# A hybrid decoder step: the values of an RWKV pair turned by two transpositions and one product, and two pairs of half-row products cut into column pieces

## The chip, the cores and the metric

The kernel runs on one core of a Trainium2 chip. The metric is device microseconds (us) for one execution of the whole program: the median of three runs, and beside it one more execution recorded by the hardware profiler, whose rows are quoted below. Less is better.

## The reference, cut to what matters

One trunk layer is computed for 256 prompt tokens and 8 x 8 sample tokens (320 columns in all), in fp32. All groups read one normalised input:

```
proj = rms_norm(x) @ w_in
y_rw = rwkv7_mix(p_rw)     # 12 heads x 64: S = S*w + (S a) b^T + v k^T ; y = S r ; then layer norm, bonus, gate
y_hg = hgrn2_mix(p_hg)     # 6 heads, state 128 x 128, S = exp(b_last) S + sum (k exp(b_last - b)) v^T
y_lru = rglru_mix(p_lru)   # 512 channels
x = x + concat(y_rw, y_hg, y_lru) @ w_out
x = x + (silu(conv(gate)) * val) @ ffn_w_down      # gate, val = rms_norm(x) @ ffn_w_up
```

In `rwkv7_mix` the decay w and the rate a come from `tanh(xw) @ rwkv_w2` and `xa @ rwkv_a2`, two products over 64 rows each. The head outputs, all new states and two final norms are returned.

## The kernel before, in words

**The stream of weight products.** Tokens lie along the columns, features on the 128 partitions. Every weight tile of 128 x 128 is used in three products, because the fp32 operands are split into a high and a low part: high weight with high input (L198), high weight with low input (L199), low weight with high input (L205). A chunk is eight such tiles: SyncE loads it into `raw` (L167), ScalarE (ACT) makes the high part `wh` (L173), VectorE (DVE) the low part `wl` (L174). There are three buffers of `raw`, `wh` and `wl` each, and chunks are split two ahead of their use. A chunk is 16 products of L198 and L199 in turn, then 8 of L205, into PSUM tile `acc`.

**The chains between them.** The three mixing groups are generators (`rwkv_operands` = queue f, `rwkv_chunks` = r, `rwkv_norm` = n, `hgrn_steps` = h, `lru_steps` = l). Each `yield` carries a delay, and `tick()` inside the weight product lets a chain go on when the planned clock has passed it. So pieces of these chains stand between the weight products on TensorE (PE), in an order that is set when the program is built. Pairs of RWKV heads (0 to 5) and HGRN heads (0 to 5) alternate, about 80 us for one of each. Within an engine everything runs strictly in the built order; the framework that records the program also chooses, by its own estimate of readiness, how the instructions of different chains lie on ACT and DVE. A chain's PSUM tiles `aux_r` are four banks used in turn: a product that takes a bank waits until the bank's last reader is done.

**The part around the change**, for pair p. PE: `L621` turns the values v of the pair (as four products of 64 columns with the identity); the norm chain of the pair before stands near it (L832 variance, L842 gate); then L631 (sample values), L640 and L647 (transpositions of BK and BKs), L656 and so on. ACT: L623 copies L621's result to `vsw`; L834 and L835 are Ln and Exp on the variance of the pair before; L934 and L935 are four Exp of the HGRN head; L632 to L634 copy the sample values to `vs` and `uv`; L642 copies the BK transposition to `bkt`, L838 finishes the norm. An ACT instruction whose function isn't in the table that is loaded has an `ACT_TABLE_LOAD` ahead of it. In pairs 1 to 5, L640's first product waits for L623 and its second for L834 (the last readers of the two banks that it takes), L647 waits for L634, and L656 for the first L642. Pair 0 has no norm chain ahead of it.

**Elsewhere.** L482 are two products over 64 rows each (rows 0 to 63 give w, rows 64 to 127 give a) of 320 columns into two banks; L1048 are two over 64 rows each of 512 columns into two banks, for the sample states of an HGRN head. In pair p, the block inverse `U` is built by 30 small DVE instructions (L611, L613), written out and read back by SyncE (L614, L615), and turned by L686. A plain fp32 product takes two PE instructions in the trace, a transposition one.

## Time and profile before

| | |
|---|---|
| three runs | 1625.08, 1626.22, 1627.49 us; median 1626.22 |
| profiled execution | 1627.56 us, of which the span from first to last instruction 1625.8 |
| granted TensorE clock, mean | 0.997 |
| busy share of the span | PE 99%, weight loads on PE 95%, DVE 60%, ACT 50%, GpSimd 9% |
| HBM | 146 GB/s over the span |

PE spans are pipelined: a weight product is shown for 0.31 us, while the next starts 0.147 us after it, so PE counts as idle only when a wait is longer than what is still in flight. Distances between starts say more than durations do. In waits and timelines, `PEld` is the loading of the stationary operand, which runs ahead of the product, and "idle before, releaser" names what ended a wait.

### The profile page before, as it was taken

Reading aid. Unit: us, or ns where it says so; the run is one execution under the profiler, and the core shown is the slowest. Engines: PE = TensorE matmul, PEld = TensorE weight load, DVE = VectorE, ACT = ScalarE, POOL = GpSimd, SP = SyncE. Lnnn points to the kernel's source line nnn. Section 1 sums busy time; section 2 is a strip of 40 time slices with the busy share of each in tenths; the row PEclk is TensorE's granted clock in tenths of the full one; section 3 lists DMA queues with packets and bytes.
Section 4 is the critical chain, followed back from the end, with each engine's and each line's share of the span. In section 5 each row is a group of like instructions: output and inputs, shape, how many; then the busy total and the mean of one; then the engine's idle time right before and its main releaser. Section 6 shows DMA issues by size and latency. Waiting matters only on the chain.

```text
span 1625.8 us, 29013 instructions
## 1 busy us (share of the span) xinstructions
PE 1601.6 (99%) x11478; PEld 1548.6 (95%) x11478; DVE 973.9 (60%) x1965; ACT 809.6 (50%) x1280; POOL 144.7 (9%) x364
## 2 busy tenths in 40 slices
PE   9999999999999999999999999999999999999996
PEld 8888989898989999999999999999999999999996
DVE  7786878777776765555555554343455555554444
ACT  7766766676766964443434343323334343344442
POOL 2101111111111300001111110000011110000000
PEclk9999999999999999999999999999999999999998
DMA  8444343444344554454445444555444444445553
GB/s 266 154 132 135 117 141 120 128 120 136 114 135 122 168 169 150 151 158 148 151 148 156 145 153 144 147 152 149 155 151 154 146 153 145 155 146 156 149 151 109
DMA packets 87791, 238.91 MB, mean 147 GB/s; under 512 B 16712, under 2 KB 31096, under 8 KB 87656
## 3 DMA queue, kind: packets, MB, share of 16 engines
q1 hardware_dynamic: 81496, 221.01, 44.4%
q0 software_dynamic: 4576, 14.16, 2.6%
q8 instruction: 90, 1.47, 0.4%
q10 hardware_dynamic: 1584, 1.89, 0.3%
q14 instruction: 45, 0.37, 0.1%
HBM read 225.66 MB, written 11.37 MB: 146 GB/s over the span
## 4 chain that ended last, share of the span: by engine, by line
PE 85%; ACT 7%; DVE 4%; DMA 2%; issue 2%; SPq 0%; POOL 0%; DVEq 0%; ACTq 0%
PE acc L198 26%; PE acc L205 26%; PE acc L199 26%; DVE wl L174 1%; PE aux_r L703 1%; PE aux_h L914 1%; ACT wh L173 1%; DMA raw<-in_w_in 1%; ACT L935 0%; ACT L893 0%; ACT L1023 0%; DVE x L1289 0%; PE aux_r L656 0%; PE aux_r L729 0%; DMA mskf<-in_msk 0%
## 5 line engine op out<-in xcount | busy, mean ns | idle before, releaser
L173 ACT CAST wh<-raw 128x1024 fp32r<-128x1024 f32 (+2 forms) x412 | 421.6, 1025 | 542.8 <-PE acc L199 338.2
L198 PE MATMUL acc<-xh,wh 128*128 128x320 f32 x2192 | 661.0, 315 | 0.0
L199 PE MATMUL acc<-xl,wh 128*128 128x320 f32 x2192 | 648.2, 309 | 0.0
L174 DVE TENSOR_TENSOR wl<-raw,wh 128x1024 fp32r<-128x1024 f32 (+2 forms) x412 | 489.9, 1190 | 224.5 <-ACT wh L173 113.1
L198 PEld LDWEIGHTS acc<-xh,wh 128*128 128x128 f32 x2192 | 411.7, 188 | 13.6 <-issue 10.7
L199 PEld LDWEIGHTS acc<-xl,wh 128*128 128x128 f32 x2192 | 411.7, 188 | 1.3
L205 PE MATMUL acc<-xh,wl 128*128 128x320 f32 x2192 | 372.6, 312 | 0.0
L205 PEld LDWEIGHTS acc<-xh,wl 128*128 128x128 f32 x2192 | 332.3, 188 | 2.8
L198 PE MATMUL acc<-hh,wh 128*128 128x320 f32 x704 | 207.9, 308 | 0.0
L199 PE MATMUL acc<-hl,wh 128*128 128x320 f32 x704 | 207.9, 308 | 0.0
L199 PEld LDWEIGHTS acc<-hl,wh 128*128 128x128 f32 x704 | 132.1, 188 | 0.0
L198 PEld LDWEIGHTS acc<-hh,wh 128*128 128x128 f32 x704 | 131.7, 187 | 0.0
L205 PE MATMUL acc<-hh,wl 128*128 128x320 f32 x704 | 118.8, 308 | 0.0
L1251 POOL COPY ncch<-fe 128x18 f32<-128x18 f32 x44 | 49.7, 1131 | 652.7 <-DVE fe L1250 652.7
L205 PEld LDWEIGHTS acc<-hh,wl 128*128 128x128 f32 x704 | 107.1, 187 | 0.0
L1261 DVE TENSOR_TENSOR fv<-acc,rstd 128x320 f32<-128x320 f32 x44 | 21.6, 492 | 98.5 <-PE acc L205 98.5
L1249 DVE TENSOR_TENSOR fe<-acc,rstd 128x256 f32<-128x256 f32 x44 | 18.7, 425 | 99.6 <-PE acc L205 99.6
L214 ACT CAST hh<-fv 128x320 fp32r<-128x320 f32 x44 | 20.3, 460 | 96.9 <-DVE fv L1263 96.9
L198 PE MATMUL acc<-yhl,wh 128*128 128x320 f32 x224 | 66.2, 310 | 0.0
L199 PE MATMUL acc<-yhl,wh 128*128 128x320 f32 x224 | 66.0, 307 | 0.0
L1256 DVE SCALAR_TENSOR_TENSOR fc<-fe,prm,fc 128x336 f32<-128x336 f32 x88 | 49.8, 566 | 1.6
L1254 ACT ACTIVATE fc<-fe,prm 128x336 f32<-128x336 f32 x44 | 29.4, 669 | 35.7 <-DVE fe L1250 35.7
(416 smaller groups left out, 1616.6 us busy)
## 6 DMA issues: line engine op xcount, KB each, us to landing
raw<-in_w_up SPq DMA_DIRECT2D x176, 512.0 KB, 3.5
raw<-in_w_in SPq DMA_DIRECT2D x100, 512.0 KB, 3.5
raw<-in_w_dn SPq DMA_DIRECT2D x64, 512.0 KB, 3.4
raw<-in_w_out SPq DMA_DIRECT2D x32, 512.0 KB, 3.6
raw<-in_w_dn SPq DMA_DIRECT2D x32, 384.0 KB, 3.0
out_s_hgrn<-hs POOLq DMA_DIRECT2D x12, 256.0 KB, 4.6
xr<-in_xT SPq DMA_DIRECT2D x16, 160.0 KB, 3.8
hs<-in_hs POOLq DMA_DIRECT2D x10, 256.0 KB, 4.2
```

The costliest lines, as they stand in the source:

```text
L173: S.copy(wh[:, ks, :], raws[n][:, ks, :])
L174: V.tensor_tensor(wl[:, ks, :], raws[n][:, ks, :], wh[:, ks, :].bitcast(F32), op=ALU.subtract)
L198: PE.matmul(ps[:, :T], wh[:, k, :], xh[k0 + k], start=st, stop=False)
L199: PE.matmul(ps[:, :T], wh[:, k, :], xl[k0 + k], start=False, stop=False)
L205: PE.matmul(ps[:, :T], wl[:, k, :], xh[k0 + k], start=False, stop=en)
L214: S.copy(xh, src)
L703: PE.matmul(ps[q, b * 64:(b + 1) * 64], lhs[q, b, q], r[q], start=True, stop=True)
L1249: V.tensor_tensor(e[:, 2:258], ps[:, 0:TP], rstd[:, 0:TP], op=ALU.mult)
L1251: G.tensor_copy(ncch[:, j], e[:, 248:EX].rearrange("p (b s) -> p b s", s=10)[:, :, 8:10])
L1254: S.activation(c[:, 0:N], e[:, 0:N], AF.Identity, scale=pc("fw", 3 * j), bias=pc("fb", j))
L1256: V.scalar_tensor_tensor(c[:, 0:N], e[:, m:m + N], pc("fw", 3 * j + m), c[:, 0:N], op0=ALU.mult, op1=ALU.add)
L1261: V.tensor_tensor(val, ps[:, :T], rstd, op=ALU.mult)
```

## The change

It does three things. (1) The values are turned by one transposition of columns 64 to 191 (128 x 128), one of columns 192 to 255 into partitions 0 to 63, and one product with the identity for columns 0 to 63 into partitions 64 to 127. The two upper blocks then lie in swapped places, so that `vsw` is filled by three copies on ACT (the lower 64 partitions at once, the upper ones block by block) in place of one. (2) L482 becomes four products of 160 columns, (3) L1048 four of 256 columns, the two row halves in turn for each column piece.

```diff
         ps_w, ps_a = aux_r(), aux_r()
-        for n, ps in enumerate((ps_w, ps_a)):
-            PE.matmul(ps[:, :T], lw[half[n], n, :], lora[half[n], :], start=True, stop=True)
+        for c in (slice(0, T // 2), slice(T // 2, T)):
+            for n, ps in enumerate((ps_w, ps_a)):
+                PE.matmul(ps[:, c], lw[half[n], n, :], lora[half[n], c], start=True, stop=True)
...
         ps = aux_r()
-        for c in range(4):
-            PE.matmul(ps[half[1 - c % 2], (c // 2) * P:(c // 2 + 1) * P], v[:, c * 64:(c + 1) * 64], ident,
-                      start=True, stop=True)
-        S.copy(flat(vsw), ps[:, 0:256])
+
+        PE.transpose(ps[:, 0:P], v[:, 64:192], ident)
+        PE.transpose(ps[lo, P:256], v[:, 192:256], ident)
+        PE.matmul(ps[hi, P:256], v[:, 0:64], ident, start=True, stop=True)
+        S.copy(flat(vsw)[lo], ps[lo, 0:256])
+        for m in range(2):
+            S.copy(vsw[hi, m, :], ps[hi, (1 - m) * P:(2 - m) * P])
         yield L_FILL
...
         pss = [aux_h(), aux_h()]
-        for q, ps in zip(half, pss):
-            PE.matmul(ps, kt[q, 2, :], flat(ex[q]), start=True, stop=True)
+
+        for c in (slice(0, TP), slice(TP, 2 * TP)):
+            for q, ps in zip(half, pss):
+                PE.matmul(ps[:, c], kt[q, 2, :], flat(ex[q])[:, c], start=True, stop=True)
```

Since the framework orders the instructions anew, more moves than these lines. Line numbers of the changed kernel are 4 higher than before in the part around the pair (L834 is now L838, L934 is L938, L640 is L644).

On ACT in pair 1, from the logarithm of the HGRN head (`b`, L893) on; `sqy` is the norm chain of pair 0, `e` and `f` are the exponentials of the head, `vsw`, `vs`, `uv` and `bkt` the copies for the pair. Before:

```order
L893 ACTIVATE b<-b,eps_t 128x320
L623 COPY vsw<-aux_r 128x256
L834 ACTIVATE sqy<-aux_r,eps_t 128x320
L935 ACT_TABLE_LOAD
L935 ACTIVATE e<-b 128x80x2
L934 ACTIVATE e<-x 128x80x2
...
L632 COPY vs<-aux_r 128x64
L633 COPY uv<-aux_r 64x64
L634 COPY uv<-aux_r 64x64
L173 CAST wh<-raw 128x1024
L838 ACTIVATE yc<-yc,prm 128x320
L642 COPY bkt<-aux_r 128x4x64 x2
```

And now, the same stretch:

```order
L897 ACTIVATE b<-b,eps_t 128x320
L625 COPY vsw<-aux_r 64x256
L627 COPY vsw<-aux_r 64x128 x2
L939 ACT_TABLE_LOAD
L939 ACTIVATE e<-b 128x80x2
L838 ACT_TABLE_LOAD
L838 ACTIVATE sqy<-aux_r,eps_t 128x320
L938 ACT_TABLE_LOAD
L938 ACTIVATE e<-x 128x80x2
...
L638 COPY uv<-aux_r 64x64
L646 COPY bkt<-aux_r 128x4x64 x2
L173 CAST wh<-raw 128x1024
```

The Ln of the norm chain (L834, now L838) has moved behind the first Exp of the head, with a table load ahead of it and one behind it; the two copies of `bkt` now stand ahead of the cast and of L838 (now L842). It is so in pairs 1 to 5; in all, ACT has 88 table loads in place of 78. Pair 0, without a norm chain, gets no load.

On PE in pair 1, the products that wait for ACT there, and what they wait for (`[waits Activation_49]`), before. `BK` and `BKs` are turned, `ARs` is multiplied with the sample state:

```order
L842 MATMUL aux_r<-sg,lw 128x320 [waits DVE_49,PE_49]
L640 MATMUL aux_r<-cst,BK 128x64 [waits Activation_49] x2
L640 MATMUL aux_r<-cst,BK 128x64 x6
...
L647 MATMUL aux_r<-cst,BKs 128x128 [waits PE_49,Activation_49]
...
L656 MATMUL aux_r<-s_1811,ARs 128x256 [waits DMASW4_49,Activation_49]
```

Nothing moved among these on PE: the same products stand at the same places of the weight stream, and they wait for the same ACT instructions (L640's second for the Ln, L647 for the last `uv` copy, L656 for the first `bkt` copy).

On PE in pair 0, where the block inverse `U` of the pair is turned (`qk` are the products of the HGRN head); the piece of the difference:

```order
 L205 MATMUL acc<-xh_248,wl 128x320
-L914 MATMUL aux_h<-qk 128x64 x2
+L690 MATMUL aux_r<-cst,U 128x128 x4
+L918 MATMUL aux_h<-qk 128x64 x2
 L198 MATMUL acc<-xh_146,wh 128x320
 L199 MATMUL acc<-xl_147,wh 128x320
 L198 MATMUL acc<-xh_150,wh 128x320
 L199 MATMUL acc<-xl_151,wh 128x320
-L686 MATMUL aux_r<-cst,U 128x128 x4
```

The turning of `U` now stands ahead of two products of the head and four weight products. On DVE, four instructions fewer stand ahead of the last step of pair 0's block inverse (one split L174 and three of the head), and on SyncE its write-out (L614) is issued one weight load earlier.

## The prediction, made before the result was known

> **What bounds the kernel now.** First the engines' shares, the chain that ended last, and one stage: 80 us from pair 1's start, that is, one RWKV pair and one HGRN head (columns: PE, PEld, DVE, ACT, GpSimd, then granted clock).

> ```profile
> PE 1601.6 (99%) x11478; PEld 1548.6 (95%) x11478; DVE 973.9 (60%) x1965; ACT 809.6 (50%) x1280; POOL 144.7 (9%) x364
> ...
> PE 85%; ACT 7%; DVE 4%; DMA 2%; issue 2%; SPq 0%; POOL 0%; DVEq 0%; ACTq 0%
> ...
> 146.00:226.00 80.00, 79.19 (x647) 71.53 (x646) 63.33 (x197) 53.72 (x109) 10.17 (x26) 1.00 0.41 126
> ```

> TensorE is the bound. In the stage it has 0.8 us that it could give back, so a pause added there goes nearly whole into the time. ACT's 50% says nothing yet; what counts is whether ACT is ahead of PE at the place of the change. The chain of waits answers that: two lines that name ACT, each five times, in five of the six pairs, and one wait of the casts.

> ```profile
> PEld aux_r L656 <- ACT bkt L642: 2.1, 5, 0.4
> ...
> PEld aux_r L647 <- ACT uv L634: 1.4, 5, 0.3
> ...
> ACT wh L173 <- PE acc L199: 338.2, 210, 4.7
> ```

> So here PE already waits for ACT, though briefly, while over the whole program ACT waits 338 us for PE. The timeline of pair 1 shows how both are true. ACT:

> ```profile
> 142.41 1.05 ACT L173 CAST wh<-raw 128x1024 fp32r<-128x1024 f32 x1 [4.75 <-PE acc L199]
> ...
> 148.82 0.56 ACT L893 ACTIVATE b<-b,eps_t 128x320 f32<-128x320 f32 x1
> 149.29 0.35 ACT L623 COPY vsw<-aux_r 128x256 f32<-128x256 f32 x1
> 149.54 0.53 ACT L834 ACTIVATE sqy<-aux_r,eps_t 128x320 f32<-128x320 f32 x1
> 150.09 1.28 ACT L935 ACT_TABLE_LOAD   x1
> 151.39 0.35 ACT L935 ACTIVATE e<-b 128x160 f32<-128x160 f32 x1
> 151.64 0.34 ACT L934 ACTIVATE e<-x 128x160 f32<-128x160 f32 x1
> ...
> 152.92 0.21 ACT L633 COPY uv<-aux_r 64x64 f32<-64x64 f32 x1
> 153.14 0.20 ACT L634 COPY uv<-aux_r 64x64 f32<-64x64 f32 x1
> 153.25 1.05 ACT L173 CAST wh<-raw 128x1024 fp32r<-128x1024 f32 x1
> ...
> 154.75 0.62 ACT L642 COPY bkt<-aux_r 128x256 f32<-128x256 f32 x2
> ```

> ACT idles 4.75 us, is let go by a weight product at 142.41, and from there runs dense to 157; it can't start sooner, whatever is idle before. PE in the same stretch:

> ```profile
> 146.67 0.31 PE L199 MATMUL acc<-xl,wh 128*128 128x320 f32 x1
> 146.91 0.66 PE L621 MATMUL aux_r<-cst,xs 128*64 128x128 f32 x8
> ...
> 147.75 0.31 PE L199 MATMUL acc<-xl,wh 128*128 128x320 f32 x1
> 147.90 0.31 PE L198 MATMUL acc<-xh,wh 128*128 128x320 f32 x1
> ...
> 151.55 0.46 PE L640 MATMUL aux_r<-cst,BK 64*128 64x64 f32 x8
> ...
> 153.07 0.30 PE L199 MATMUL acc<-xl,wh 128*128 128x320 f32 x1
> 153.40 0.44 PE L647 MATMUL aux_r<-cst,BKs 128*128 128x128 f32 x2
> ...
> 155.16 1.13 PE L656 MATMUL aux_r<-s,ARs 128*128 128x256 f32 x4
> ...
> 159.10 0.34 PE L673 MATMUL aux_r<-cst,AR 64*128 64x64 f32 x4
> ```

> L634 ends at 153.34 and L647 starts at 153.40: no slack. The first of the two L642 ends about 155.06 (154.75 and half of 0.62), L656 starts at 155.16: no slack. L640's second product needs L834, which ends at 150.07: slack 1.48. Weight products start 0.15 apart (147.75, 147.90).

> **ACT's new order, pairs 1 to 5.** From 149.29 on, with distances taken from the rows. The vsw copies: 0.25 for the first (149.29 to 149.54), 0.22 for each of the two small ones (as L633 to L634), so they end near 150.0. The first load, 1.28 plus 0.02, puts L935 at 151.33. Now L834 needs the other table back: L935's 0.35, and a load to 153.0; L834 to 153.53; a third load, so that the first L934 starts at 154.85 instead of 151.64. From there to the end of L634 is as before, 153.34 - 151.64 = 1.70: it ends at 156.55, 3.2 later. (Check: two loads of 1.30, 0.45 for the copies, 0.12 because L935 must end before a load; 3.2.) Nothing covers it: ACT has no idle between 142.41 and there, and it cannot start earlier.

> What this does to PE: L640's second product can start at 153.55 instead of 151.55, a pause of 2.0. From its start to L647 unhindered are 1.67 (151.55 to 153.07, and 0.15), so PE arrives at 155.2 and waits until 156.6: 1.4 more, of which 0.2 to 0.3 was waited before, together 3.2 at this point. From L647 to L656 were 1.76, with a wait for L642 in it. L642 now stands ahead of the cast, ends soon after 156.55, and isn't waited for: minus 0.3, and about 0.1 of refilling after it. Net 3.2 - 0.4 = **2.8 us per pair, 14.0 for five**. Bounds: 2.4 if pauses hide more of the changes of shape beside them, 3.2 if the wait at L656 stays in another form.

> [...]

> The cast that now waits behind bkt comes about 4 us later. It makes the chunk after next: there are three wh buffers, a chunk lasts over 3.5 us on PE (24 products of 0.15), and so at least 7 us are in hand; casts also waited 1.6 us on average for PE. I take 0, and price that cover under the rivals.

> **The turn of the values.** L621 with its edges takes 147.75 - 146.67 less two weight products, 0.79. Eight instructions of 128 columns before, two at a time, are four turns; now a transposition alone, then a transposition beside a product of two, are three. One turn, from L647 in pair 0, below: two transpositions in 72.98 - 72.46 - 0.29 = 0.23, so 0.115 each. I take 0.12 saved per pair, between 0 and 0.56 (the whole turn as cheap as L647's two). In pairs 1 to 5 it only brings PE earlier to the pause at L640: worth nothing. In pair 0 it counts.

> **The pieces of L482 and L1048.**

> ```profile
> 47.03 0.81 PE L482 MATMUL aux_r<-lora,lw 64*128 64x320 f32 x4
> ...
> 138.70 1.13 PE L1048 MATMUL aux_h<-hex,kt 64*128 64x512 f32 x4
> ...
> 72.46 0.31 PE L199 MATMUL acc<-xl,wh 128*128 128x320 f32 x1
> 72.61 0.38 PE L647 MATMUL aux_r<-cst,BKs 128*128 128x128 f32 x2
> ...
> 72.98 0.30 PE L199 MATMUL acc<-xl,wh 128*128 128x320 f32 x1
> ```

> A full-array product of 320 columns takes 0.15, and a plain fp32 one moves its columns at half that pace twice over (128 columns in 0.115 at L647 against 0.06): 320 columns are 0.27 per instruction, 512 are 0.43. Four in a row would need 1.07 and 1.71; the groups last 0.81 and 1.13. Two in parallel need 0.54 and 0.86 and a start of 0.27. So the two row halves already run beside each other, and smaller pieces change nothing but eight more instructions per pair: 0 to +0.1 in all, I take +0.1.

> **Pair 0.** No norm chain, so no added load.

> ```profile
> 69.95 0.88 DVE L593 TENSOR_TENSOR mt<-aux_r,msk 128x128 f32<-128x128 f32 x4
> ...
> 70.60 0.81 PE L640 MATMUL aux_r<-cst,BK 64*128 64x64 f32 x8
> ...
> 88.41 1.22 DVE L174 TENSOR_TENSOR wl<-raw,wh 128x1024 fp32r<-128x1024 f32 x1
> ...
> 95.23 0.55 PE L914 MATMUL aux_h<-qk 128*128 128x64 f32 x4
> ...
> 97.41 0.66 PE L686 MATMUL aux_r<-cst,U 128*128 128x128 f32 x4 [0.99 <-DMA U<-du]
> ```

> L640 takes 0.81 here and 0.46 in pair 1: its second product waits for a bank that L593 reads until 70.83. In the new order that bank's last reader is the vsw copy, done before: -0.35, and -0.12 for the turn. At 97.41 PE waits for U. DVE has four instructions fewer ahead of U's last step, one of 1.22 and three of about 0.2 apart, so U lands about 1.7 earlier; and work moved behind the turn of U (four weight products, 0.59, and two products of L914, about 0.36) leaves PE there 0.95 earlier. Landing sets the time: -1.7 + 0.95 = -0.75. If U's chain keeps its own time, the 0.47 ahead are lost in that wait, otherwise they add. I take **-1.0** for pair 0, between -1.2 and, if U lands no sooner, +0.95.

> **The sum.** 14.0 + 0.1 - 1.0 = +13.1 on the profiled execution's 1627.6: 1640.7. That execution lies 1.3 above the median of 1626.2, so the median forecast is **1639.3**. With the bounds of the terms: 5 x 2.4 + 0 - 1.2 = +10.8 to 5 x 3.2 + 0.1 + 0.95 = +17.1, that is 1637 to 1643.3.

> **Rivals.**

> *The other side: the loads stay hidden.* One mechanism: ACT reaches L893 over 2.8 us earlier than the distances say, by a start ahead of 142.41. For it: 50% busy, and 4.75 us idle just before. Against: that idle is ended by PE, ahead of anything the change touches, and from there ACT is dense. It decides where ACT is 3 us earlier; PE would keep only pair 0's -1.0 and five turns of 0.12: 1624.7, within 0.2% (3.25 us, about what a measurement of this kernel can tell from no change). 8%, a quarter of it below that band by some further gain.

> *DVE is late next.* The low half of the delayed cast (L174) stands on DVE ahead of L658, on which PE leans.

> ```profile
> 157.21 0.68 DVE L658 TENSOR_TENSOR tmp<-aux_r,cst 128x512 f32<-128x512 f32 x1
> ```

> After: the cast ends near 158.1, L174 (1.2, as in pair 0) at 159.35, L839 and one small step to 159.95, L658 ends at 160.6. L673 takes the bank that L658 reads, and PE arrives there at 159.10 + 2.8 = 161.9: slack 1.3. U's small steps behind L174 come 3.9 later for PE's 2.8, so U loses 1.1. If either slack is overrun by 1 us in five pairs, +5: 1644.3. 12%.

> *A slow clock after the pauses.* PE's first products, after a pause of 1.1 us, were 0.27 apart (8.20, 8.47) and later 0.15.

> ```profile
> 7.18 0.64 PE L307 MATMUL aux_r<-xh,wh 128*128 128x320 f32 x1 [1.12 <-ACT xh L217]
> ...
> 8.20 0.47 PE L307 MATMUL aux_r<-xh,wh 128*128 128x320 f32 x1
> 8.47 0.47 PE L308 MATMUL aux_r<-xl,wh 128*128 128x320 f32 x1
> ```

> If the two pauses of 2.0 and 1.4 in 5 us bring that back, some 15 products cost 0.12 each more, 1.8 per pair: 1648. Against it: the stage from 146 has pauses in it too, of 0.3 to 0.4, and its clock reads 1.00. [...] 4%.

> *The pieces do gain.* [...] 4%.

> **How the numbers follow.** The forecast, with its own range 1636 to 1643, has 72%. The rivals' 8, 12, 4 and 4 make the rest. The range for 8 in 10 takes the bounds, and reaches into DVE's case above and into a smaller price of the loads below: 1633 to 1645. Slower by over 0.2% is all but the first rival: 0.92, less 0.02 for a mixture of small loads and gains; faster 0.03; within 0.2% 0.07.

> **What the profile after would show.** Ten more table loads. In pairs 1 to 5: PE waiting about 2.0 at the BK transpositions for the Ln of the norm chain, about 1.4 at the BKs ones for the last uv copy, and the wait for bkt gone. The two piece groups as long as before. In pair 0 the wait for U at 0.4 or less. PE's busy time is unchanged within 2 us, the span is not. I am wrong if ACT has idle time between the Ln of the head and the uv copies; if the pauses at those two places sum to under 2 us per pair; or if new waits for DVE or for U stand behind them.

## The result, and the profile after

The changed kernel takes **1652.15 us** (median of four runs, 1648.81 to 1653.11) against 1625.79 for the kernel before on the same chip: 1.0157 times as long, 95% interval 1.0139 to 1.0175. The forecast was 1639.3, with a range up to 1645. The direction was right, the size half of what came.

The page of the changed kernel, then its list of PE's waits (total, times, longest):

```profile
PE 1612.0 (98%) x11502; PEld 1562.7 (95%) x11502; DVE 974.2 (59%) x1965; ACT 824.6 (50%) x1302; POOL 149.0 (9%) x364
```
```profile
PE aux_r L644 <- ACT sqy L838: 9.0, 5, 1.8
PE aux_r L651 <- ACT uv L638: 4.5, 5, 1.2
PE aux_r L707 <- DVE T L699: 2.9, 5, 0.6
```

PE's busy time has grown by 10 us, though its program has only a few small instructions more. That is the first sign that work on PE became slower, not only later. ACT in pair 1, where the Ln (L838) stands between two exponentials:

```profile
148.28 0.35 ACT L625 COPY vsw<-aux_r 64x256 f32<-64x256 f32 x1
148.64 0.42 ACT L627 COPY vsw<-aux_r 64x128 f32<-64x128 f32 x2
149.08 1.28 ACT L939 ACT_TABLE_LOAD   x1
150.37 0.35 ACT L939 ACTIVATE e<-b 128x160 f32<-128x160 f32 x1
150.74 1.28 ACT L838 ACT_TABLE_LOAD   x1
152.04 0.53 ACT L838 ACTIVATE sqy<-aux_r,eps_t 128x320 f32<-128x320 f32 x1
152.58 1.28 ACT L938 ACT_TABLE_LOAD   x1
153.88 0.35 ACT L938 ACTIVATE e<-x 128x160 f32<-128x160 f32 x1
...
155.38 0.20 ACT L638 COPY uv<-aux_r 64x64 f32<-64x64 f32 x1
155.49 0.64 ACT L646 COPY bkt<-aux_r 128x256 f32<-128x256 f32 x2
```

Three loads in a row where one stood, each 1.28 with 0.02 around it. From the first vsw copy (148.28) to the end of L638 (155.58) are 7.30 us; before, from 149.29 to 153.34, 4.05. That is 3.25 more. PE in the same stretch:

```profile
152.62 0.46 PE L644 MATMUL aux_r<-cst,BK 64*128 64x64 f32 x7 [1.81 <-ACT sqy L838]
...
155.64 0.69 PE L651 MATMUL aux_r<-cst,BKs 128*128 128x128 f32 x2 [1.20 <-ACT uv L638]
...
156.39 0.47 PE L199 MATMUL acc<-xl,wh 128*128 128x320 f32 x1
156.66 0.47 PE L198 MATMUL acc<-xh,wh 128*128 128x320 f32 x1
...
158.25 1.91 PE L660 MATMUL aux_r<-s,ARs 128*128 128x256 f32 x4
...
161.85 0.70 PE L667 MATMUL aux_r<-rk,cst 128*128 128x320 f32 x2
...
163.65 0.34 PE L677 MATMUL aux_r<-cst,AR 64*128 64x64 f32 x4
```

The two pauses are where they were foreseen. But from 155.6 on weight products stand 0.27 apart instead of 0.147, and L660 lasts 1.91 instead of 1.13. The granted clock shows why: it falls to one half at 154.72 and is back at 161.55, 6.83 us later. In pair 4 it falls at 410.72 and is back at 414.13, 3.41 later, half as long. So here is the same stretch in windows of 3.41 us (PE busy first; the granted clock is the third number from the end):

```profile
151.44:154.86 3.42, 1.82 (x15) 1.50 (x15) 0.60 (x2) 3.38 (x7) 0.01 (x1) 0.98 0.19 58
154.86:158.27 3.41, 2.63 (x11) 2.64 (x12) 2.41 (x6) 3.23 (x10) 0.00 (x0) 0.50 0.02 5
158.27:161.68 3.41, 3.41 (x12) 3.04 (x12) 2.10 (x9) 1.28 (x2) 0.00 (x0) 0.52 0.49 154
161.68:165.10 3.42, 3.42 (x37) 2.93 (x36) 3.37 (x9) 1.14 (x4) 1.46 (x1) 1.00 0.00 0
```

A window in which PE is busy for 1.82 of 3.42 is followed by one at half clock; that one holds 2.63 busy, and the next is slow too; that one is full, and the clock is back. The slow stretches of pairs 2 and 3 begin at these rows:

```profile
240.19 0.47 PE L198 MATMUL acc<-xh,wh 128*128 128x320 f32 x1
...
325.41 0.47 PE L198 MATMUL acc<-xh,wh 128*128 128x320 f32 x1
```

They are 85.22 apart, 25 times 3.41. This alone proves little, since the kernel itself repeats after 85.56 there (BK at 236.68 and at 322.24). The granted clock says more: in pairs 1 to 5 it falls at 154.72, 240.05, 325.38, 410.72 and 496.05, each 85.33 after the one before, while BK starts 4.2, 3.4, 3.1, 3.0 and 4.6 ahead of these points. So the clock changes on a grid of 3.41 us, and this grid runs free of the kernel.

**Where the 25.2 us are.** The two profiled executions differ by 1652.77 - 1627.56 = 25.2. Starts of the BK and AR transpositions (L640 and L673 before, L644 and L677 after) cut each pair in two; us from mark to mark:

| | pair 1 | 2 | 3 | 4 | 5 |
|---|---|---|---|---|---|
| BK to AR, before | 7.55 | 7.54 | 7.54 | 7.54 | 7.54 |
| BK to AR, after | 13.11 | 12.76 | 12.65 | 10.98 | 11.70 |
| AR to the next BK, before | 72.33 | 72.11 | 72.13 | 72.11 | |
| AR to the next BK, after | 73.03 | 72.80 | 72.79 | 72.80 | |

The first part is 23.5 longer in all, the second 2.75, and everything ahead of pair 1's BK is 1.0 shorter: 25.2. Of the 23.5, the pauses are 14.2 (L651 comes 3.25 later against BK in each of the five pairs, and 0.42 of it is given back before AR, as the kernel exp_first below shows at full clock); 9.3 remain for the slow clock: 2.7, 2.4, 2.3, 0.6 and 1.3, by two slow windows in each of pairs 1 to 3 and one in pairs 4 and 5.

### The profile page after: what moved, and what is told of

Its sections match the earlier page's. It is cut to its first block, busy times and chain, and to the rows that moved or that the text cites. A ratio compares the mean times of both kernels' runs of the same rounds, so it can differ in the third digit from the quotient of the medians.

```text
span 1651.0 us, 29057 instructions
## 1 busy us (share of the span) xinstructions
PE 1612.0 (98%) x11502; PEld 1562.7 (95%) x11502; DVE 974.2 (59%) x1965; ACT 824.6 (50%) x1302; POOL 149.0 (9%) x364
## 4 chain that ended last, share of the span: by engine, by line
PE 85%; ACT 8%; DVE 4%; issue 1%; DMA 1%; SPq 0%; DVEq 0%; ACTq 0%
PE acc L198 26%; PE acc L199 26%; PE acc L205 25%; DVE wl L174 1%; PE aux_h L918 1%; ACT wh L173 1%; PE aux_r L707 1%; DMA raw<-in_w_in 1%; PE aux_r L660 0%; ACT L938 0%; ACT L838 0%; ACT L939 0%; ACT L897 0%; ACT L1027 0%; ACT L505 0%
## 5 line engine op out<-in xcount | busy, mean ns | idle before, releaser
L173 ACT CAST wh<-raw 128x1024 fp32r<-128x1024 f32 (+2 forms) x412 | 421.6, 1025 | 561.3 <-PE acc L199 354.9
L198 PE MATMUL acc<-xh,wh 128*128 128x320 f32 x2192 | 665.4, 317 | 0.0
L199 PE MATMUL acc<-xl,wh 128*128 128x320 f32 x2192 | 652.4, 311 | 0.0
L174 DVE TENSOR_TENSOR wl<-raw,wh 128x1024 fp32r<-128x1024 f32 (+2 forms) x412 | 489.9, 1190 | 230.7 <-ACT wh L173 115.3
L198 PEld LDWEIGHTS acc<-xh,wh 128*128 128x128 f32 x2192 | 414.6, 189 | 9.4 <-issue 6.5
L199 PEld LDWEIGHTS acc<-xl,wh 128*128 128x128 f32 x2192 | 415.1, 189 | 1.3
L198 PE MATMUL acc<-hh,wh 128*128 128x320 f32 x704 | 207.9, 308 | 0.0
L199 PE MATMUL acc<-hl,wh 128*128 128x320 f32 x704 | 207.9, 308 | 0.0
L199 PEld LDWEIGHTS acc<-hl,wh 128*128 128x128 f32 x704 | 132.2, 188 | 0.0
L198 PEld LDWEIGHTS acc<-hh,wh 128*128 128x128 f32 x704 | 131.7, 187 | 0.0
L198 PE MATMUL acc<-yhl,wh 128*128 128x320 f32 x224 | 66.2, 310 | 0.0
L199 PE MATMUL acc<-yhl,wh 128*128 128x320 f32 x224 | 66.0, 307 | 0.0
```

The source lines that it names most:

```text
L173: S.copy(wh[:, ks, :], raws[n][:, ks, :])
L174: V.tensor_tensor(wl[:, ks, :], raws[n][:, ks, :], wh[:, ks, :].bitcast(F32), op=ALU.subtract)
L198: PE.matmul(ps[:, :T], wh[:, k, :], xh[k0 + k], start=st, stop=False)
L199: PE.matmul(ps[:, :T], wh[:, k, :], xl[k0 + k], start=False, stop=False)
```

## The experiments

**The order of the exponentials.** [exp_first] One order is enforced on ScalarE, and nothing else moves:

```diff
-        for t0, t1, sc in ((e0, e1, 1.0), (f0, f1, -1.0)):
-            S.activation(t0, x0, AF.Exp, scale=sc)
-            S.activation(t1, b1, AF.Exp, scale=sc)
+        first = S.activation(e0, x0, AF.Exp, scale=1.0)
+        with tc.issue_after(first.ins):
+            S.activation(e1, b1, AF.Exp, scale=1.0)
+            S.activation(f0, x0, AF.Exp, scale=-1.0)
+            S.activation(f1, b1, AF.Exp, scale=-1.0)
```

> The changed kernel with one order enforced on ScalarE: the first exponential of the HGRN head is the one of x, which is ready after the Ln of the norm chain; all else stands as in the changed kernel. 78 table loads instead of 88. Theory A (the ten added loads are the whole loss: they make PE pause, and the pauses drop its clock): no pause over 0.5 us at the BK and BKs transpositions, no slow clock, and the gain of pair 0 (-1.0) plus the vanished wait for bkt in five pairs (up to -2.0) stay: 1623 to 1625.5. Theory B (the new turn or the pieces cost time by themselves, on PE or through late DVE work): the loads gone give back only the pauses, and 1635 or more stays.

Measured: 1629.30, 1.0016 (1.0007 to 1.0024). 23 of the loss are gone with ten table loads, no product is slow, BK to AR takes 7.67 in every pair. But it is above the expected 1625.5, and still slower than before. Its waits name what is left:

```profile
PE aux_r L707 <- DVE T L699: 2.9, 5, 0.6
PE aux_r L651 <- ACT uv L638: 2.8, 5, 0.6
```

The second is in the 7.67. The first is new, and it is the 0.7 of the second part of each pair. DVE in this kernel, pair 1, and then DVE and PE in the kernel before at the same place:

```profile
185.50 0.55 DVE L511 SCALAR_TENSOR_TENSOR kn<-xs,prm,kn 128x320 f32<-128x320 f32 x1 [2.25 <-ACT kn L506]
185.96 0.44 DVE L699 COPY_PREDICATED U<-msk,aux_r 128x256 f32<-128x256 uint8 x1
186.30 0.48 DVE L513 SCALAR_TENSOR_TENSOR nb<-kn,a 128x320 f32<-128x320 f32 x1
186.70 0.42 DVE L699 COPY_PREDICATED T<-msk,aux_r 128x256 f32<-128x256 uint8 x1
```
```profile
185.16 0.43 DVE L695 COPY_PREDICATED U<-msk,aux_r 128x256 f32<-128x256 uint8 x1 [1.18 <-PE aux_r L703]
186.40 0.55 DVE L510 SCALAR_TENSOR_TENSOR kn<-xs,prm,kn 128x320 f32<-128x320 f32 x1 [0.80 <-ACT kn L505]
186.86 0.43 DVE L695 COPY_PREDICATED T<-msk,aux_r 128x256 f32<-128x256 uint8 x1
...
187.81 0.68 PE L703 MATMUL aux_r<-T,mt 64*64 64x64 f32 x16
```

Before, U is updated while DVE waits for kn from ACT. Now U stands behind that wait, and T behind U and nb; T ends at 187.12 and PE starts L707 at 187.26, 0.58 idle.

**T ahead of U.** [t_first] On top of exp_first; only DVE's order differs.

```diff
-            update(Us[:, 0:4, :], f"u{h}", 1, ps_u)
             if h == 16:
                 update(Ts, "t16", 0, ps_t)
+            update(Us[:, 0:4, :], f"u{h}", 1, ps_u)
```

> The kernel of exp_first (no added loads) with the two masked copies behind the products U,Z and Z,U in turned order, T ahead of U; only DVE's order differs, by the product nb that T no longer stands behind. Theory A (in exp_first the 0.8 us per pair between the turn of U and the next pair are PE's wait for T, made by the new order on DVE): no wait for T, 0.6 to 0.8 less in each of five pairs, 1625 to 1626.5. Theory B (the wait only moves to U or to the next step of that chain): 1628 to 1630 as in exp_first.

Measured: 1627.07, 1.0004 (0.9995 to 1.0013); between the two theories. AR to the next BK is 72.43 instead of 72.78 in pairs 2 to 4, so about half of the 0.7 is back; the rest is a wait for U of 0.3, which is late now in T's place. So this wait comes from the order on DVE.

**Which part of the change.** [turn_only] The kernel before with the turn alone:

> The kernel before with only the turn of the values changed; it has 88 table loads too. Theory A: the whole loss is here, 1648 to 1653, with slow products behind the second pause in each of five pairs. Theory B (the pieces carry part of it): clearly below 1648.

Measured: 1651.14, 1.0146 (1.0131 to 1.0162): the whole loss, with slow products in each of the five pairs. [pieces_only] The kernel before with both groups of pieces alone:

> The kernel before with only L482 and L1048 cut into column pieces; 78 table loads. Theory A (the halves of the rows already run beside each other): the two groups last 0.81 and 1.13 as before, and the time is that of before within 1.0, as far as moved instructions elsewhere don't decide. [...]

Measured: 1625.98, 0.9995 (0.9986 to 1.0004). Nothing. In the changed kernel the two groups last exactly as long as before:

```profile
46.86 0.81 PE L483 MATMUL aux_r<-lora,lw 64*128 64x160 f32 x8
...
137.67 1.13 PE L1054 MATMUL aux_h<-hex,kt 64*128 64x256 f32 x8
```

[three_copies] The kernel before, with its four products, but with three copies:

```diff
-        S.copy(flat(vsw), ps[:, 0:256])
+        S.copy(flat(vsw)[lo], ps[lo, 0:256])
+        for m in range(2):
+            S.copy(vsw[hi, m, :], ps[hi, m * P:(m + 1) * P])
```

> The kernel before, its turn of the values by four products and the pieces left as they were, but vsw filled by three copies (the lower 64 partitions at once, the upper ones block by block) as in the changed kernel. It has 88 table loads. Theory A (the three copies on ScalarE are what moves the Ln behind an exponential; turn and pieces are not needed for the loss): 1647 to 1653, with pauses of about 1.8 and 1.2 us and slow products in most of five pairs. Theory B (the turn on PE has a part in it): below 1645.

Measured: 1651.91, 1.0157 (1.0141 to 1.0173): the whole loss, without turn and pieces, and with the same three waits:

```profile
PE aux_r L642 <- ACT sqy L836: 9.1, 5, 1.8
PE aux_r L649 <- ACT uv L636: 4.5, 5, 1.2
PE aux_r L705 <- DVE T L697: 2.9, 5, 0.6
```

[one_copy] The reverse: turn and pieces, with one copy.

> The changed kernel, turn and pieces included, with one copy of all 256 columns into vsw in place of three (the two blocks of the upper partitions then stand exchanged, so that the values of these rows go to the wrong heads). 78 table loads. Theory A: nothing of the loss is left, 1624.5 to 1628, no slow products. Theory B (the turn costs time by itself): 1632 or more.

Measured: 1628.05, 1.0011 (1.0002 to 1.0020), just above the expected range. No slow products and no pause at BK or BKs; the wait for T is still there:

```profile
PE aux_r L705 <- DVE T L697: 2.9, 5, 0.6
```

So two copies more, 0.45 us of ACT, put the Ln behind an exponential in the order that is fixed when the program is built, and the loads follow from that order. The late T comes with the turn even with one copy, and with the three copies even without the turn; with the pieces alone it does not.

**Is it the clock?** [fill] The ten loads stay; products that nothing reads fill the pauses.

```diff
         pss = [aux_r(), aux_r()]
+        for _ in range(4 if p else 0):
+            PE.matmul(pss[0][:, 256:512], ident, cst[:, 0:256], start=True, stop=True)
...
+        for _ in range(3 if p else 0):
+            PE.matmul(pss[0][:, 256:512], ident, cst[:, 0:256], start=True, stop=True)
```

> The changed kernel with its ten added loads, and in pairs 1 to 5 seven plain products that nothing reads: four ahead of the BK transpositions (4 x 2 x 0.215 = 1.7 us) and three behind them (1.3 us), into unused columns of a bank that PE holds there anyway. They fill the two pauses with work and don't shorten them. Theory A (pauses cost about 13, the clock that falls after them about 12): products stay 0.147 apart, clock 0.997 or more, 1638 to 1642. Theory B (the second half of the loss is DVE and ACT work that comes late behind the pauses, and the clock only goes along): 1650 or more.

Measured: 1643.17, 1.0097 (1.0083 to 1.0111): 9.0 below the changed kernel, with more work on PE. The same two stretches as above now read:

```profile
151.44:154.86 3.42, 3.04 (x21) 2.60 (x19) 2.91 (x6) 3.40 (x12) 0.00 (x0) 1.00 0.03 5
154.86:158.27 3.41, 3.41 (x20) 3.15 (x21) 3.38 (x20) 1.68 (x8) 0.00 (x0) 1.00 0.53 154
```

It ends 1 us above the expected band: the order on ACT shifted so that a wait of 0.4 for bkt came back in five pairs, while four of the five waits for T went. The 9.0 are therefore not the clock alone to the tenth; that there was no slow product is the firm part.

**Which pause?** [fill_first] and [fill_second] Only the four products, or only the three.

> The changed kernel, ten added loads, with idle products in the first pause only (four, 1.7 us); the second pause of 1.4 stands alone. Theory A (it takes over 1.5 us idle within one window): clock stays full, 1641 to 1645 like the kernel with both pauses filled. Theory B (any pause over 1 us drops it): 1648 or more.

Measured: 1641.01, 1.0092 (1.0078 to 1.0106), no slow product; the second pause stands alone, and wherever the grid lies, 1.2 of idle leaves a window over 60% busy:

```profile
PE aux_r L655 <- ACT uv L638: 6.0, 5, 1.2
```

> The changed kernel, ten added loads, with idle products behind the first pause only (three, 1.3 us), so that the second pause is filled; the first, 1.8 to 2.0 us, stands alone. Theory A (over 1.5 us idle within one window of 3.4 drops the clock, and a next window that is full brings it back): slow for one window where the pause lies in one window, not where an edge cuts it; 1644 to 1650. Theory B (the two pauses have to come together): 1641 to 1644.

Measured: 1641.92, 1.0093 (1.0080 to 1.0107). In the profile, slow products in pairs 1 and 4 alone, for one window each. Pair 1, then pair 2, on the grid that the slow stretch of pair 1 sets:

```profile
148.11:151.52 3.41, 1.61 (x13) 1.28 (x13) 0.00 (x0) 3.35 (x5) 0.54 (x1) 1.00 0.33 70
151.52:154.93 3.41, 3.41 (x15) 3.15 (x13) 2.32 (x6) 3.39 (x11) 0.00 (x0) 0.51 0.00 0
...
230.02:233.43 3.41, 2.64 (x21) 1.76 (x19) 0.66 (x2) 3.35 (x7) 0.54 (x1) 1.00 0.45 104
233.43:236.85 3.42, 2.39 (x18) 2.17 (x19) 0.75 (x3) 3.38 (x8) 0.00 (x0) 1.00 0.23 62
...
315.36:318.78 3.42, 1.79 (x14) 1.57 (x14) 0.15 (x1) 3.38 (x6) 0.46 (x1) 1.00 0.30 66
318.78:322.19 3.41, 3.41 (x24) 3.18 (x22) 2.68 (x6) 3.39 (x12) 0.00 (x0) 1.00 0.00 0
```

The same pause of 1.8: in pair 1 it lies in one window, which is 1.61 busy (47%), and the next is slow. In pair 2 an edge cuts it, the windows are 2.64 and 2.39 busy (77 and 70%), and nothing happens. So one pause was enough, and where the grid lay against it decided. The last two rows are pair 3, where an edge cuts only a little of the pause off: the window is 1.79 busy, and still nothing happens. With the grid set more exactly, by the points at which the granted clock changes (151.57 and 400.74 in this run), it is 1.84 busy (54%). In the changed kernel windows that were 1.82 and 1.83 busy (pairs 1 and 5) were followed by half the clock. If the busy share of a window were all that decides, its limit would lie close to 54%. But at the start of the changed kernel a window that was 2.02 of 3.42 busy (59%, 4.53 to 7.95) was followed by half the clock too, so what else has a part in it isn't shown.

Only two pairs of five were hit, so that the time lies below the expected 1644, in the range of theory B. The slow products in pairs 1 and 4, where one pause stood alone, speak against that theory all the same. The pairs at full clock (2, 3 and 5) take 10.38 to 10.41 from BK to AR: as much as 7.54 before and 2.84 for the pauses, which bears out the shares of the clock worked out above.

[pause3] No added loads (t_first), but the first exponential of the head done four times in pairs 1 to 5:

> The kernel of t_first with the first exponential of the HGRN head done four times instead of once in pairs 1 to 5: ScalarE is about 1.1 us later, PE's order stays, and one pause of some 1.6 us stands at the BKs transpositions. Theory A (the clock falls when a window of about 3.4 us that runs free of the kernel holds enough idle time, at least the 1.6 or so of the shortest case in the changed kernel): at the edge, products slow in none or some of the five pairs; 1631 without, up to 1640 with it. [...]

Measured: 1630.67, 1.0025 (1.0014 to 1.0036), no slow product; the pause was 1.3:

```profile
PE aux_r L651 <- ACT uv L638: 6.3, 5, 1.3
```

Against t_first the three exponentials more cost PE 0.7 per pair (BK to AR 8.36 for 7.67), and no slow clock. As the pause came out shorter than meant, this run did not reach the edge.

**A version that beats both?** [bkt_dve] pieces_only, with the first bkt copy on VectorE in pairs 1 to 5.

```diff
-            S.copy(bkt[:, :, e, :], c64(pss[e][:, 0:256]))
+            (S.copy if e or not p else V.tensor_copy)(bkt[:, :, e, :], c64(pss[e][:, 0:256]))
```

> The kernel of pieces_only with one of the two copies of bkt on VectorE in pairs 1 to 5, where VectorE sits idle for about half a microsecond; PE's order is unchanged. If the wait of 0.4 us for bkt on ScalarE is what holds PE in five pairs: 1.5 to 2 less than pieces_only, 1624 to 1625. If the next wait (for the other bkt copy or the split of the weights behind it on VectorE) takes its place: 1626 as before.

Measured: 1624.68, 0.9992 (0.9982 to 1.0001). BK to AR shrinks from 7.55 to 7.12, 0.4 in each of five pairs as worked out, but 2 us in 1626 are not clear of the measurement.

## Why the prediction was wrong, step by step

- **ACT's order: right.** Ten more loads of 1.28, and L638 3.25 later against PE in pair 1; forecast 3.2.
- **The pauses: right.** 1.8 of idle at BK and 1.2 at BKs in the list of waits, where the forecast of 2.0 and 1.4 counted from starts; the wait for bkt gone; 14.2 in five pairs, forecast 14.0.
- **The clock: the step that failed.** The sum had 0 for it. The rival "A slow clock after the pauses" had the effect and nearly the price (1.8 per pair, 9; measured 9.3), but 4% of the chance, and so the range ended short of it. With 9.3 for the clock and the 2.75 of the next point, the forecast of 1639.3 would have been 1651.4. That the rival's price came so near is partly luck: it took the same for every pair, and the pairs paid 0.6 to 2.7; it asked for both pauses, and one was enough (fill_second). Its evidence was PE's first products of the kernel, 0.27 apart at 8.20 and 0.15 from 10.57 on; the trace of before has no record of the clock until 10.51 and reads 1.00 there, so that these rows alone don't show a clock falling after a pause. In the changed kernel PE's products at 8.20 are 0.27 apart too, and there the clock reads 0.50 from 7.95 to 11.36. The reason given against the rival, the stage's clock of 1.00, was read from pauses of 0.3 to 0.4, which say nothing of pauses of 2; here a window that was 47 or 53% busy was followed by half the clock.
- **"DVE is late next": also 0 in the sum, and the place was another.** As a rival it had 12% and 1 us per pair, 5 in all. At the two places that it named (the bank that L658 reads, and U) PE has no wait for DVE in pairs 1 to 5. The wait came where the order of T on DVE wasn't looked at: 0.7 in each of four distances, 2.75. A new wait for DVE was one of the prediction's own signs of being wrong.
- **Pair 0: right in its parts, in sum partly by luck.** From BK to BKs it takes 1.67 instead of 2.01, -0.34 (forecast -0.35). From AR to the next BK it takes 72.79 instead of 73.72, -0.93 (forecast -0.75): the wait of 0.99 for U is gone. Together that is -1.3, just beyond the bound of -1.2. The sum of -1.0 came out because BK of pair 0 starts 0.27 later, at 70.87 instead of 70.60; in the other runs it starts anywhere from 67.94 to 71.94. The two rows now:

```profile
70.87 0.46 PE L644 MATMUL aux_r<-cst,BK 64*128 64x64 f32 x8
...
95.16 0.62 PE L690 MATMUL aux_r<-cst,U 128*128 128x128 f32 x4
```

- **The turn: mis-sized, 0 for 0.12.** From the last weight product ahead of it to the second behind it are 68.06 - 66.99 = 1.07 in pair 0, and were 1.08:

```profile
66.99 0.31 PE L199 MATMUL acc<-xl,wh 128*128 128x320 f32 x1
67.14 0.27 PE L622 MATMUL aux_r<-cst,xs 128*128 128x128 f32 x1
...
67.45 0.43 PE L624 MATMUL aux_r<-cst,xs 128*64 128x128 f32 x2
...
68.06 0.31 PE L199 MATMUL acc<-xl,wh 128*128 128x320 f32 x1
```

- **The pieces: right,** 0. That the halves run beside each other was read from lengths: groups of 0.81 and 1.13, too short for one half after the other, and in the changed kernel as long as before. (The prediction's 0.27 and 0.43 per instruction are a little short: 0.115 for 128 columns gives 0.29 and 0.46. The groups of 0.81 and 1.13 are then all the more too short for one instruction after the other.)

The parts add up: 14.2 + 9.3 + 2.75 - 1.0 = 25.2.

## What to carry to other kernels

When a change adds instructions to an engine that others wait for, look at the order that results and not only at their length: 0.45 us of copies cost 25 us, by table loads that the order brings, by the slow clock behind the pauses that they make, and by the places of DVE instructions. Where PE will pause for over a microsecond, count how much of a window of 3.41 us it will be busy: at about half or below (here 47 to 53%), add the slow products behind it, and give that case its weight. The grid ran free of this kernel, so count a pause as if it lay in one window. And fix a fragile order explicitly: one enforced order took back 23 us.
